# Last expert tile of a decoder block: sums moved between the halves of its gate and up products, the final scaling moved mostly to VectorE, and a drain on GpSimd's queue

## The chip, the cores and the metric

The kernel runs on one core of one Trainium2 chip. The metric is device time in microseconds: 1058.45 us is the median of three runs of the kernel before (1056.13 to 1059.59). In the text PE is TensorE, DVE is VectorE, ACT is ScalarE, POOL is GpSimd and SP is SyncE, which issues most of the DMAs. A name with a q behind it (POOLq, SPq) is the engine's queue, where instructions stand that set registers, wait, drain or issue DMAs.

## The reference

One decoder block for 512 tokens of 1024 channels: two attention branches side by side, then 64 routed experts and a shared one, then a root-mean-square norm. What the change touches is the end of the routed experts and the norm:

```python
def expert_block(xs):
    tok, g, e = xs
    xb = x_pad[tok]
    hb = jax.nn.silu(xb @ w_exp_gate[e]) * (xb @ w_exp_up[e])
    return (hb @ w_exp_down[e]) * g[:, None]
...
routed = jax.ops.segment_sum(yb.reshape(n_rows, D), row_tok, num_segments=T + 1)[:T]
...
x = x + gate_f * moe_ffn(...)
return rms_norm(x, g_final)
```

## The kernel before

The rows of all experts are packed into 33 tiles of 128 rows (a tile holds 32 to 128 rows of an expert). For each tile POOL gathers the 128 token rows with an indirect DMA (`fetch`, L1218) and copies their token numbers (`tokf`, L1222). PE turns the gathered rows over (`turn`), and `first` (L1242) multiplies them with the gate and up weights of the tile's experts, eight channel blocks k, all into one PSUM buffer `gu`. `hide` makes the hidden values from it (ACT's Silu, L1250, and a product on DVE, L1251), `turn_hidden` turns them over on PE (L1257) and copies them out of PSUM on ACT (L1258). `expert_out` is called for the two halves of the 1024 channels: PE's products with the down weights into a PSUM buffer `y` (L1274), DVE's scaling by gate value (`ys`, L1278), then the split of the result into a high part on ACT (`yH`, L155) and a low part on DVE (`yL`, L158).

The segment sum is a matrix product too: `spread` makes a one-hot matrix `oht` of tokens by rows, and `combine` (L1298 and L1299, 128x512 each) multiplies it with `yH` and `yL` for each block i of 128 tokens and each half of the channels; DVE adds the result to the running sum `acc` in SBUF (L1300). Tiles are combined in pairs; in front of the last tile one tile stands uncombined (`full`).

Last tile, before (L1393 to L1460). `first` runs through, the tile in front is combined for the first half of the channels, and the hidden values are turned. For the second half of the channels nothing goes through `acc` in SBUF: `seed(i)` puts `acc` into a PSUM buffer `fo` by a product with the identity (L1418) and adds the tile in front to it (L1412, L1413); the four seeds stand around the two halves of the last tile's down products. Then, for each block i of 128 tokens, `add_last(i)` combines the last tile into `acc` for the first half, squares and sums it on ACT (L1433), adds the last tile to `fo` for the second half, squares and sums that on ACT too, multiplies the first half with the final gain on DVE (L1440), adds up the two sums of squares (`fs`, L1442), and raises them to the power -1/2 on POOL (L1443). `store_last(i)` scales the second half from PSUM on DVE (L1446), the first half on ACT (L1448), and SP stores both to HBM (L1450). `store_last(i - 1)` is called behind `add_last(i)`.

The order of the instructions on PE and SP is the order of the code. That on DVE, ACT and POOL is chosen by a scheduler, which goes by its own estimate of when inputs are ready; once chosen it is fixed, and each engine works through its own queue in that order. Behind the last store stands a loop for experts that overflowed their rows (L1485); its count is read from the data, and here it is not entered. Then come the waits for all DMAs and the drains and barriers in which a program ends (recorded under L1517).

Of the kernel before, what the change touches and what calls it, by code (L numbers as in the profile page):

```python
# [10 lines left out]
F32 = mybir.dt.float32  # L11
# [75 lines left out]
def build(ctx, tc, a, out, dbg=None):  # L87
# [1128 lines left out]

    def fetch(T, x):
# [4 lines left out]
        follow(G.tensor_copy(tokf, tb[:, T, 0:1]), last[0])  # L1222
# [169 lines left out]

    T = TILES - 1  # L1393
# [10 lines left out]
    hid = hide(*first([ents], xT))  # L1404
    combine(full, cols=halves[:1])
    hT = turn_hidden(hid)
    sums = []

    def part(i, states, c, start, stop):
        t = slice(i * 128, (i + 1) * 128)  # L1410
        for q, (oht, yH, yL) in enumerate(states):
            PE.matmul(sums[i], oht[:, t], yH[:, c], start=start and q == 0, stop=False)  # L1412
            PE.matmul(sums[i], oht[:, t], yL[:, c], start=False, stop=stop and q == len(states) - 1)  # L1413

    def seed(i):
        tag, bufs = (("tr", 2), ("tr", 2), ("cb", 1), ("gu", GUB))[i]
        sums.append(mo_p.tile([128, S], F32, name="fo", tag=tag, bufs=bufs))
        PE.matmul(sums[i], ident, acc[:, i, halves[1]], start=True, stop=False)  # L1418
        part(i, full, halves[1], False, False)

    seed(0)
    state = spread(toks.pop(T))
    expert_out(0, T, ents, hT, state, WIDE)
    seed(1)
    expert_out(1, T, ents, hT, state, WIDE)
    seed(2)
    seed(3)
    outs = [xg[T % 3], xg[(T - 1) % 3]]
    outs += [work.tile([128, D], F32, name="yo", tag=tag, bufs=n) for tag, n in (("xT", 1), ("yH", 2))]

    def square(i, n, src):

        return A.activation(outs[i][:, halves[1]], src, AF.Square, scale=1.0 / 32.0, accum_out=fs[:, n, i:i + 1])  # L1433

    def add_last(i):
        combine([state], [i], ((("ht", 1), ("gu", GUB), ("ht", 1), ("y", 2))[i],), halves[:1])
        square(i, 0, acc[:, i, halves[0]])
        part(i, [state], halves[1], False, True)
        square(i, 1, sums[i])
        V.tensor_tensor(outs[i][:, halves[0]], acc[:, i, halves[0]], gfin[:, halves[0]], ALU.mult)  # L1440
        p = slice(i, i + 1)
# [3 lines left out]
    def store_last(i):  # L1445
        V.scalar_tensor_tensor(outs[i][:, halves[1]], sums[i], fs[:, 1, i:i + 1], gfin[:, halves[1]], op0=ALU.mult,  # L1446
                               op1=ALU.mult)
        scaled = A.mul(outs[i][:, halves[0]], outs[i][:, halves[0]], fs[:, 1, i:i + 1])  # L1448
        for c in halves[::-1]:
            SP.dma_start(outr[:, i, c], outs[i][:, c])  # L1450
        return scaled

    for i in range(NT):
        add_last(i)
        if i:
            store_last(i - 1)
# [73 lines left out]
```

## Time and profile before

| what | value |
| --- | --- |
| median of the runs, us | 1058.45 |
| lowest and highest run, us | 1056.13, 1059.59 |
| profiled execution, us | 1053.89 |
| its span, first to last instruction, us | 1052.2 |
| busy share PE, DVE, ACT, POOL | 95%, 55%, 30%, 15% |
| mean granted clock of PE, share of full speed | 0.981 |

The profiled execution is faster than each of the three runs; it has 1.7 us outside its span. A busy time is the sum over an engine's instructions. The chain of waits follows the work that ended last back to what released it. The 40 slices of the page show PE at 0.9 or more through nearly the whole span; the last slice, which holds the stores and the end of the program, has PE at 0.3.

### The profile page before, as it was taken

How to read it: one execution, taken by the hardware profiler on the slowest of the kernel's cores; microseconds unless marked ns; L12 is line 12 of the kernel's file. 1: busy time of each engine (PE TensorE's matmuls, PEld its weight loads, DVE VectorE, ACT ScalarE, POOL GpSimd, SP SyncE). 2: the span in 40 equal slices, each digit the busy share in tenths (PEclk: the TensorE clock that was granted, in tenths of full speed). 3: DMA queues.
4: the chain of work that ended last, by engine and by line, in shares of the span. 5: the costliest groups of instructions: out<-in, count | busy, mean ns of one | idle time of the engine just before them, and what ended most of it. 6: DMA issues, size and time to landing. Idle time of an engine off the chain costs nothing.

```text
span 1052.2 us, 16301 instructions
## 1 busy us (share of the span) xinstructions
PE 1001.2 (95%) x5904; PEld 602.8 (57%) x5904; DVE 575.1 (55%) x1151; ACT 320.5 (30%) x701; POOL 156.1 (15%) x209
## 2 busy tenths in 40 slices
PE   8999999998989988998899999999999999999993
PEld 7678667776756668975434444454344444434442
DVE  3568676477748653676344455454445455445454
ACT  3445553232225532430222222122212212222214
POOL 1513001000031265145200000000000000000000
PEclk8999999998999999999999999999999999999997
DMA  8942104599660276715699999999999999999782
GB/s 236 309 148 57 57 1 133 195 287 272 183 211 21 81 252 243 249 62 187 229 416 414 417 417 369 382 417 413 389 381 369 381 417 410 377 376 415 310 313 81
DMA packets 104467, 286.11 MB, mean 272 GB/s; under 512 B 18241, under 2 KB 65049, under 8 KB 80322
## 3 DMA queue, kind: packets, MB, share of 16 engines
q1 hardware_dynamic: 97458, 270.33, 69.0%
q0 software_dynamic: 5648, 12.63, 3.2%
q10 hardware_dynamic: 1280, 2.10, 0.7%
q8 instruction: 47, 0.77, 0.3%
q14 instruction: 34, 0.28, 0.1%
HBM read 282.46 MB, written 4.66 MB: 273 GB/s over the span
## 4 chain that ended last, share of the span: by engine, by line
PE 80%; DVE 6%; DMA 5%; SPq 3%; issue 2%; POOL 2%; ACT 1%; POOLq 0%; ACTq 0%; DVEq 0%
PE gu L1242 22%; PE y L1274 11%; PE o L150 6%; PE o L149 6%; PE o L151 6%; PE o L1298 6%; PE o L1299 5%; PE tp L1229 3%; PE sp L570 3%; PE oc L594 2%; PE tp L582 2%; DMA wm<-in_w_mod_dram 1%; PE og L1027 1%; PE tp L1257 1%; DMA w<-in_w_mod_dram 1%
## 5 line engine op out<-in xcount | busy, mean ns | idle before, releaser
L1242 PE MATMUL gu<-gu,xT 128*32 128x512 f32 (+1 forms) x1664 | 233.4, 594 | 0.0
L1242 PEld LDWEIGHTS gu<-gu,xT 128*32 128x32 f32 (+1 forms) x1664 | 69.1, 117 | 150.7 <-issue 137.0
L1274 PE MATMUL y<-dn,hid 128*32 128x512 f32 (+1 forms) x832 | 120.5, 596 | 0.0
L1251 DVE TENSOR_TENSOR hid<-hid,gu 128x256 f32<-128x256 f32 x33 | 13.9, 421 | 164.9 <-ACT hid L1250 164.9
L1298 PE MATMUL o<-yH,oht 128*128 128x512 f32 x256 | 101.9, 398 | 0.7 <-DVE acc L1300 0.7
L1300 DVE TENSOR_TENSOR acc<-acc,o 128x512 f32<-128x512 f32 x136 | 91.0, 686 | 17.4 <-PE o L1299 17.4
L1299 PE MATMUL o<-yL,oht 128*128 128x512 f32 x256 | 100.1, 391 | 0.0
L150 PE MATMUL o<-hH,wL 128*128 128x512 f32 x208 | 83.4, 401 | 1.2 <-DVE wL L158 1.2
L149 PE MATMUL o<-hH,wH 128*128 128x512 f32 x208 | 83.2, 400 | 0.0
L151 PE MATMUL o<-hL,wH 128*128 128x512 f32 x208 | 82.4, 396 | 0.0
L155 ACT CAST yH<-ys 128x512 fp32r<-128x512 f32 (+1 forms) x68 | 41.2, 607 | 109.3 <-DVE ys L1278 109.3
L158 DVE TENSOR_TENSOR yL<-ys,yH 128x512 fp32r<-128x512 f32 (+1 forms) x68 | 45.9, 677 | 43.5 <-ACT yH L155 43.3
L1274 PEld LDWEIGHTS y<-dn,hid 128*32 128x32 f32 (+1 forms) x832 | 32.5, 117 | 63.8 <-issue 54.6
L1250 ACT ACTIVATE hid<-gu 128x256 f32<-128x256 f32 x33 | 12.7, 386 | 180.4 <-PE gu L1242 180.4
L1278 DVE SCALAR_TENSOR_TENSOR ys<-y,tb,gmb 128x512 f32<-128x512 f32 (+1 forms) x68 | 49.8, 735 | 30.8 <-PE y L1274 26.8
L1218 POOL DMA_INDIRECT xg<-h2d,tb x22 | 22.2, 1011 | 274.5 <-PE tp L1229 191.5
L1298 PEld LDWEIGHTS o<-yH,oht 128*128 128x128 f32 x256 | 48.1, 188 | 12.9 <-DVE acc L1300 2.3
L898 ACT ACTIVATE xT<-tp,ab 128x128 f32<-128x128 f32 x132 | 49.8, 457 | 14.0 <-PE tp L1229 12.4
L1299 PEld LDWEIGHTS o<-yL,oht 128*128 128x128 f32 x256 | 48.1, 188 | 9.4
L900 DVE TENSOR_SCALAR xT<-tp,ab 128x128 f32<-128x128 f32 x132 | 45.2, 405 | 10.2 <-ACT xT L898 7.4
L149 PEld LDWEIGHTS o<-hH,wH 128*128 128x128 f32 x208 | 39.5, 190 | 12.0 <-issue 1.9
L150 PEld LDWEIGHTS o<-hH,wL 128*128 128x128 f32 x208 | 39.6, 191 | 11.4 <-DVE wL L158 1.8
(384 smaller groups left out, 1673.5 us busy)
## 6 DMA issues: line engine op xcount, KB each, us to landing
gu<-in_w_exp_gate_dram SPq DMA_DIRECT2D x63, 1024.0 KB
gu<-in_w_exp_up_dram SPq DMA_DIRECT2D x63, 1024.0 KB
dn<-in_w_exp_down_dram SPq DMA_DIRECT2D x60, 1024.0 KB
w<-in_w_mod_dram SPq DMA_DIRECT2D x32, 512.0 KB
w<-in_w_in_dram SPq DMA_DIRECT2D x13, 1024.0 KB
wm<-in_w_mod_dram SPq DMA_DIRECT2D x16, 512.0 KB
wraw<-in_w_out_dram SPq DMA_DIRECT2D x12, 512.0 KB
dn<-in_w_exp_down_dram SPq DMA_DIRECT2D x8, 512.0 KB
```

Source lines behind the costliest of these rows:

```text
L149: PE.matmul(o, l[0], r[0], start=start, stop=False)
L150: PE.matmul(o, l[1], r[0], start=False, stop=False)
L151: return PE.matmul(o, l[0], r[1], start=False, stop=stop)
L158: return le.tensor_tensor(L, src, f(H), ALU.subtract)
L898: A.activation(out, src, AF.Identity, bias=ab2[:, 1, k:k + 1], scale=ab2[:, 0, k:k + 1])
L900: V.tensor_scalar(out, src, ab2[:, 0, k:k + 1], ab2[:, 1, k:k + 1], op0=ALU.mult, op1=ALU.add)
L1242: last[0] = PE.matmul(gu[lo:lo + n], xT[:, k, lo:lo + n], w[:, :, k], start=(k == 0), stop=(k == KD - 1))
L1274: last[0] = PE.matmul(y[lo:lo + m], hT[:, j, lo:lo + m], w[:, j, c], start=(j == 0), stop=(j == 1))
L1278: V.scalar_tensor_tensor(ys[:, b], y[:, b], f(tb[:, T, 1:2]), gfb[:, c][:, b], op0=ALU.mult, op1=ALU.mult)
L1298: m = PE.matmul(o, oht[:, i * 128:(i + 1) * 128], yH[:, c], start=(q == 0), stop=False)
L1299: PE.matmul(o, oht[:, i * 128:(i + 1) * 128], yL[:, c], start=False, stop=(q == len(state) - 1))
L1300: d = V.tensor_tensor(acc[:, i, c], acc[:, i, c], o, ALU.add)
```

## The change

Four things are changed, all in the last tile.

- `first` is called twice for the last tile, for k 0 to 3 and for k 4 to 7, into the same PSUM buffer. Between the calls the tile in front is combined for the first half of the channels; behind the second call it is combined for the second half too, now also through `acc` in SBUF (`combine`, with DVE's additions).
- The seeds with their two products each are gone from between the down products. Each block's `fo` now gets `acc` by the identity and then the last tile's two products, all behind the down products of both halves; the four combinations of the first half stand in front of all of these.
- In `store_last` the first half of blocks 0 to 2 is scaled on DVE in one instruction with the final gain, in place of a product on DVE and a scaling on ACT; block 3 keeps the old form. Stores of blocks 0 to 2 go out first half first. The scheduler is switched off for DVE, ACT and POOL behind the down products, so the order there is that of the code.
- A drain is put on POOL's queue behind the last gather's copy of token numbers.

```diff
@@ -1214,12 +1214,15 @@
         q, e = late.pop(0)
         WT[q][1] = load_dn(where[q], e)
 
+    last_fetch = [None]
+
     def fetch(T, x):
         last[0] = G.indirect_dma_start(out=x, out_offset=None, in_=h2d,
                              in_offset=bass.IndirectOffsetOnAxis(ap=tb[:, T, 0:1], axis=0),
                              bounds_check=S - 1, oob_is_err=False)
         tokf = work.tile([128, 1], F32, name="tokf", bufs=6)
-        follow(G.tensor_copy(tokf, tb[:, T, 0:1]), last[0])
+        last_fetch[0] = G.tensor_copy(tokf, tb[:, T, 0:1])
+        follow(last_fetch[0], last[0])
         return tokf
 
     def turn(x, xT, parts=range(2)):
@@ -1390,6 +1393,7 @@
 
 
 
+
     T = TILES - 1
     ents, xT = todo.pop(T)
     late_dn = []
@@ -1401,60 +1405,63 @@
             SP.dma_start(to[:, :, c], src[:, :, c])
     fs = work.tile([128, 2, NT], F32, name="fs")
     outr = out[0].rearrange("(i p) d -> p i d", p=128)
-    hid = hide(*first([ents], xT))
+    dr = G.drain()
+    follow(dr, last_fetch[0])
+    gu, = first([ents], xT, range(0, 4))
     combine(full, cols=halves[:1])
+    hid = hide(*first([ents], xT, range(4, KD), gu))
+    combine(full, cols=halves[1:])
     hT = turn_hidden(hid)
-    sums = []
-
-    def part(i, states, c, start, stop):
-        t = slice(i * 128, (i + 1) * 128)
-        for q, (oht, yH, yL) in enumerate(states):
-            PE.matmul(sums[i], oht[:, t], yH[:, c], start=start and q == 0, stop=False)
-            PE.matmul(sums[i], oht[:, t], yL[:, c], start=False, stop=stop and q == len(states) - 1)
-
-    def seed(i):
-        tag, bufs = (("tr", 2), ("tr", 2), ("cb", 1), ("gu", GUB))[i]
-        sums.append(mo_p.tile([128, S], F32, name="fo", tag=tag, bufs=bufs))
-        PE.matmul(sums[i], ident, acc[:, i, halves[1]], start=True, stop=False)
-        part(i, full, halves[1], False, False)
-
-    seed(0)
     state = spread(toks.pop(T))
-    expert_out(0, T, ents, hT, state, WIDE)
-    seed(1)
-    expert_out(1, T, ents, hT, state, WIDE)
-    seed(2)
-    seed(3)
+    for n in range(2):
+        expert_out(n, T, ents, hT, state, WIDE)
+    oht, yH, yL = state
     outs = [xg[T % 3], xg[(T - 1) % 3]]
     outs += [work.tile([128, D], F32, name="yo", tag=tag, bufs=n) for tag, n in (("xT", 1), ("yH", 2))]
+    sums = []
 
     def square(i, n, src):
 
-        return A.activation(outs[i][:, halves[1]], src, AF.Square, scale=1.0 / 32.0, accum_out=fs[:, n, i:i + 1])
+        A.activation(outs[i][:, halves[1]], src, AF.Square, scale=1.0 / 32.0, accum_out=fs[:, n, i:i + 1])
 
     def add_last(i):
-        combine([state], [i], ((("ht", 1), ("gu", GUB), ("ht", 1), ("y", 2))[i],), halves[:1])
+        combine([state], [i], ((("cb", 1), ("gu", GUB), ("ht", 1), ("gu", GUB))[i],), halves[:1])
         square(i, 0, acc[:, i, halves[0]])
-        part(i, [state], halves[1], False, True)
+
+    def sum_last(i):
+        c, t, p = halves[1], slice(i * 128, (i + 1) * 128), slice(i, i + 1)
+        sums.append(mo_p.tile([128, S], F32, name="fo", tag=("tr", "tr", "y", "y")[i]))
+        PE.matmul(sums[i], ident, acc[:, i, c], start=True, stop=False)
+        PE.matmul(sums[i], oht[:, t], yH[:, c], start=False, stop=False)
+        PE.matmul(sums[i], oht[:, t], yL[:, c], start=False, stop=True)
         square(i, 1, sums[i])
-        V.tensor_tensor(outs[i][:, halves[0]], acc[:, i, halves[0]], gfin[:, halves[0]], ALU.mult)
-        p = slice(i, i + 1)
+        if i == NT - 1:
+            V.tensor_tensor(outs[i][:, halves[0]], acc[:, i, halves[0]], gfin[:, halves[0]], ALU.mult)
         V.scalar_tensor_tensor(fs[:, 0, p], fs[:, 0, p], EPS, fs[:, 1, p], op0=ALU.add, op1=ALU.add)
         G.tensor_tensor(fs[:, 1, p], fs[:, 0, p], mh[:, 0:1], ALU.pow)
 
     def store_last(i):
-        V.scalar_tensor_tensor(outs[i][:, halves[1]], sums[i], fs[:, 1, i:i + 1], gfin[:, halves[1]], op0=ALU.mult,
-                               op1=ALU.mult)
-        scaled = A.mul(outs[i][:, halves[0]], outs[i][:, halves[0]], fs[:, 1, i:i + 1])
-        for c in halves[::-1]:
+        r, c = fs[:, 1, i:i + 1], halves[0]
+        if i == NT - 1:
+            A.mul(outs[i][:, c], outs[i][:, c], r)
+        else:
+            V.scalar_tensor_tensor(outs[i][:, c], acc[:, i, c], r, gfin[:, c], op0=ALU.mult, op1=ALU.mult)
+        c = halves[1]
+        scaled = V.scalar_tensor_tensor(outs[i][:, c], sums[i], r, gfin[:, c], op0=ALU.mult, op1=ALU.mult)
+        for c in halves if i < NT - 1 else halves[::-1]:
             SP.dma_start(outr[:, i, c], outs[i][:, c])
         return scaled
 
+    tail_order = tc.manual_schedule(engines={getattr(mybir.EngineType, e) for e in MAN})
+    tail_order.__enter__()
     for i in range(NT):
         add_last(i)
+    for i in range(NT):
+        sum_last(i)
         if i:
             store_last(i - 1)
     scaled = store_last(NT - 1)
+    tail_order.__exit__(None, None, None)
     order.__exit__(None, None, None)
     for i in range(NT):
         follow(A.copy(acc[:, i, halves[1]], sums[i]), scaled)
```

The first place is on PE, around the turn of the hidden values (tp) and the down products (y) of the last tile; o is `combine`, fo the sums of the second half. Before:

```order
L1299 MATMUL o<-yL,oht 128x512
L1257 MATMUL tp<-ident,hid 128x128 x2
L1418 MATMUL fo<-acc,ident 128x512
L1412 MATMUL fo<-yH,oht 128x512
L1413 MATMUL fo<-yL,oht 128x512
L1274 MATMUL y<-dn,hid 32x512 x8
L1418 MATMUL fo<-acc,ident 128x512
```

In the changed kernel, at the same place on PE, with the last product of `combine` in front of it and the first two of the next behind it:

```order
L1302 MATMUL o<-yL,oht 128x512
L1260 MATMUL tp<-ident,hid 128x128 x2
L1277 MATMUL y<-dn,hid 32x512 x16
L1301 MATMUL o<-yH,oht 128x512
L1302 MATMUL o<-yL,oht 128x512
```

The three products that stood between the turn and the down products are gone, and the down products of both halves now follow each other.

The second place is on DVE, from the last addition to `acc` on: fs is the sums of squares, hs, xg1 and the two yo are the output rows of blocks 0 to 3 (yo_9624 and yo_9625 before, yo_9625 and yo_9626 in the changed kernel), xg0 holds the final gain. Before, where the scheduler chose:

```order
L1442 SCALAR_TENSOR_TENSOR fs_9515<-fs_9515 128x1
L1440 TENSOR_TENSOR xg1_3453<-acc_3448,xg0_3452 128x512
L1446 SCALAR_TENSOR_TENSOR hs_3451<-fo_9572,fs_9515,xg0_3452 128x512
L1440 TENSOR_TENSOR yo_9624<-acc_3448,xg0_3452 128x512
L1442 SCALAR_TENSOR_TENSOR fs_9515<-fs_9515 128x1
L1300 TENSOR_TENSOR acc_3448<-acc_3448,o_9667 128x512
L1442 SCALAR_TENSOR_TENSOR fs_9515<-fs_9515 128x1
L1446 SCALAR_TENSOR_TENSOR xg1_3453<-fo_9596,fs_9515,xg0_3452 128x512
L1440 TENSOR_TENSOR yo_9625<-acc_3448,xg0_3452 128x512
L1446 SCALAR_TENSOR_TENSOR yo_9624<-fo_9616,fs_9515,xg0_3452 128x512
```

In the changed kernel, on DVE from its last addition to `acc` to its last scaling:

```order
L1303 TENSOR_TENSOR acc_3448<-acc_3448,o_9644 128x512
L1440 SCALAR_TENSOR_TENSOR fs_9515<-fs_9515 128x1 x2
L1448 SCALAR_TENSOR_TENSOR hs_3451<-acc_3448,fs_9515,xg0_3452 128x512
L1450 SCALAR_TENSOR_TENSOR hs_3451<-fo_9649,fs_9515,xg0_3452 128x512
L1440 SCALAR_TENSOR_TENSOR fs_9515<-fs_9515 128x1
L1448 SCALAR_TENSOR_TENSOR xg1_3453<-acc_3448,fs_9515,xg0_3452 128x512
L1450 SCALAR_TENSOR_TENSOR xg1_3453<-fo_9656,fs_9515,xg0_3452 128x512
L1439 TENSOR_TENSOR yo_9626<-acc_3448,xg0_3452 128x512
L1440 SCALAR_TENSOR_TENSOR fs_9515<-fs_9515 128x1
L1448 SCALAR_TENSOR_TENSOR yo_9625<-acc_3448,fs_9515,xg0_3452 128x512
L1450 SCALAR_TENSOR_TENSOR yo_9625<-fo_9667,fs_9515,xg0_3452 128x512
L1450 SCALAR_TENSOR_TENSOR yo_9626<-fo_9678,fs_9515,xg0_3452 128x512
```

The last addition to `acc` (o_9667 before, o_9644 now) has moved in front of all scalings, and two scalings of each of blocks 0 to 2 stand together, behind the sum of squares of the next block.

## Rows read from the trace of the kernel before

**Rows 1.** Busy time by stretch: PE, PEld, DVE, ACT, POOL, clock, DMA share, GB/s.
```profile
1035.00:1040.00 5.00, 0.82 (x4) 0.36 (x2) 4.53 (x11) 4.33 (x13) 2.04 (x3) 1.00 0.29 108
1040.00:1041.00 1.00, 0.00 (x0) 0.00 (x0) 0.53 (x1) 1.00 (x3) 0.00 (x0) 0.74 0.88 334
```

**Rows 2.** Timeline of the last block: start us, us, engine, line, operation, what came before.
```profile
1040.37 0.58 ACT L1433 ACTIVATE yo<-fo 128x512 f32<-128x512 f32 x1
1040.85 0.19 ACT L1433 ACTIVATION_READ_ACCUMULATOR yo<-fo 128x1 f32 x1
1041.07 0.16 DVE L1442 SCALAR_TENSOR_TENSOR fs<-fs 128x1 f32<-128x1 f32 x1 [0.55 <-ACT yo L1433]
1041.32 0.55 POOL L1443 TENSOR_TENSOR fs<-fs,mh 128x1 f32<-128x1 f32 x1 [2.17 <-DVE fs L1442]
1041.90 0.75 DVE L1446 SCALAR_TENSOR_TENSOR yo<-fo,fs,xg 128x512 f32<-128x512 f32 x1 [0.66 <-POOL fs L1443]
```

**Rows 3.** Line 1517, end of the program: times in ns min/median/max, first and last start.
```profile
L1517 POOLq DRAIN  x3: 40/103/5063, 1046.2 to 1051.8; - x3
L1517 SPq DRAIN  x3: 7/7/113, 1046.9 to 1051.8; - x3
```

**Rows 4.** Line 1511, start of the program.
```profile
L1511 POOLq INC_SWDGE_SEM  x1: 27/27/27, 0.2 to 0.2; - x1
L1511 POOLq DRAIN  x1: 169/169/169, 0.4 to 0.4; - x1
```

**Rows 5.** Page, part 3: packets, MB and share of the queue that POOL issues to.
```profile
q0 software_dynamic: 5648, 12.63, 3.2%
```

**Rows 6.** Line 1485, the loop that isn't entered.
```profile
L1485 POOLq INC_SWDGE_SEM  x1: 1404/1404/1404, 1042.4 to 1042.4; - x1
```

**Rows 7.** Timeline of POOL, last gather and first power.
```profile
946.28 1.01 POOL L1218 DMA_INDIRECT hs<-h2d,tb  x1 [10.77 <-PE tp L1229]
...
1035.45 0.95 POOL L1443 TENSOR_TENSOR fs<-fs,mh 128x1 f32<-128x1 f32 x1 [87.97 <-DVE fs L1442]
```

**Rows 8.** Chain of waits, last tile: start us, us, engine, tile, line.
```profile
1013.42 6.87 PE gu L1242 x64
1020.28 0.43 PE o L1298
1020.71 0.23 PE o L1299
...
1022.57 0.22 PE tp L1257 x2
1022.79 0.86 PE fo L1418 x2
...
1024.11 1.85 PE y L1274 x16
1025.97 1.06 PE fo L1418 x2
```

**Rows 9.** Timeline, DVE and ACT beside these products.
```profile
1021.11 2.47 DVE L1300 TENSOR_TENSOR acc<-acc,o 128x512 f32<-128x512 f32 x4
1022.83 0.37 ACT L1258 COPY hid<-tp 128x256 f32<-128x256 f32 x1 [2.09 <-PE tp L1257]
1026.04 0.88 DVE L1278 SCALAR_TENSOR_TENSOR ys<-y,tb,gmb 128x256 f32<-128x256 f32 x2 [2.46 <-PE y L1274]
1027.05 0.76 DVE L158 TENSOR_TENSOR yL<-ys,yH 128x256 fp32r<-128x256 f32 x2
```

**Rows 10.** Timeline, pace of ACT's squares and of DVE's scalings and products.
```profile
1035.37 0.62 ACT L1433 ACTIVATE yo<-acc 128x512 f32<-128x512 f32 x1
...
1035.98 0.58 ACT L1433 ACTIVATE xg<-fo 128x512 f32<-128x512 f32 x1
...
1038.52 0.75 DVE L1446 SCALAR_TENSOR_TENSOR xg<-fo,fs,xg 128x512 f32<-128x512 f32 x1
...
1039.18 0.68 DVE L1440 TENSOR_TENSOR yo<-acc,xg 128x512 f32<-128x512 f32 x1
```

## The prediction

> **What bounds the kernel now.** I read the busy time by stretch first. Up to the last tile PE has work in every microsecond, and the change leaves the amount of that work as it is, so what can be won lies behind PE's last product. The reader is to see in [rows 1] that PE has 0.82 us of work left at 1035, that DVE (4.53 of 5 us) and ACT (4.33 of 5 us) are then nearly full, and that from 1040 on little runs at all. The timeline of the last block [rows 2] shows how the results end: square, its accumulator, sum on DVE, power on POOL, last scaling, done at 1041.90 + 0.75 = 1042.65. But the span ends at 1052.2, 9.5 us later. So I looked at the line on which the program ends [rows 3]: POOL's queue holds a drain of 5.06 us. SP's drain, the other engine's end that can be read there, starts at 1046.9 and takes 0.11. POOL's first drain starts at 1046.2 and so ends at 1051.26, about 4.25 us behind SP. The barrier that follows waits for all engines, so the end of the program waits for that drain, and the remaining 0.9 us of barriers come behind it.
>
> There are thus two terms: the tail from PE's products to the last store, and POOL's drain.
>
> **The change part by part.**
>
> *PE.* The number of products is the same: 64 rows of gate and up, 16 of the tile in front, 16 + 16 down, 16 of the last tile, 4 identities. What moves is where PE changes between narrow products (32 wide) and wide ones. In [rows 8] the first wide product behind narrow ones costs 0.43 for 0.23, so 0.20; the same shows in 1.06 for an identity behind y against 0.86 elsewhere. Narrow ones behind wide ones: 16 rows of y take 1.85, while 16 at the pace of gate and up (6.87 / 64 = 0.107) take 1.72, so 0.13. Before there are three changes to wide and two back; afterwards three and two. Nothing is won or lost there.
>
> The times then go: gate and up, first half, from 1013.42, 3.43, to 1016.85. Eight sums, 0.20 + 8 x 0.23 = 2.04, to 1018.9. Second half 0.13 + 3.43, to 1022.45. The next eight sums stand where before eight stood, right behind gate and up and beside the same Silu and product; there they took from 1020.28 to 1022.57, 2.29 with their small stall, so they end at 1024.75. The turn of the hidden values, 0.22, ends at 1024.97. Now comes the one new wait on PE: the copy on ACT that took 0.37 and started 0.04 behind the turn [rows 9] was covered by a seed (0.86 and two products); this cover is gone, so the down products start at about 1025.4, 0.4 later than they could. Queued behind them are all sums of the last tile. They run 0.13 + 2 x 1.72 = 3.57, to 1028.97. The first half's high and low parts were ready 1.84 behind its product (1025.97 to 1027.81 in [rows 8, 9]), so at 1025.4 + 1.85 + 1.84 = 1029.1, and the four combinations (0.20 + 8 x 0.23) run to 1031.0. Each block's `fo` then costs 0.86 + 2 x 0.23 = 1.32: they end at 1032.3, 1033.65, 1034.95 and 1036.3. PE is done at 1035.8 before [rows 1], so PE ends 0.5 later.
>
> *DVE, in front of the tail.* Four additions are new. Four of them take 2.47 [rows 9] and run beside the sums and the down products: they start 0.83 behind the end of gate and up as before (1020.28 to 1021.11), so at 1023.3, and end at 1025.8, 1.4 before the first down product is done. They cost nothing; without that cover they would cost 2.5. The last four end later: DVE's two scalings of the second half run from 1029.0 to 1029.9, the first addition to 1030.6 (0.62 each), the low parts to 1031.35 (0.76), three additions to 1033.25.
>
> *ACT.* It loses three scalings. Its queue now holds the four squares of the first half, then the four of `fo`. The fourth starts at 1033.3, when the last addition is done. Squares follow each other at 0.61 (1035.37 to 1035.98, [rows 10]), so block 0's second square starts at 1033.9, block 1's at 1034.5. A square starts 0.70 before its sum on DVE (1040.37 to 1041.07, [rows 2]): sums at 1034.6 and 1035.2. Block 0's power starts at 1034.85 and takes 0.95, as the first one does [rows 7], and the first scaling starts at 1035.8.
>
> *DVE, the tail.* From there it is DVE's queue that ends last. Scalings follow each other at 0.66 (1038.52 to 1039.18, [rows 10]). Two scalings 1.32, a sum 0.16, two scalings 1.32, block 3's product 0.66, a sum 0.16, two scalings 1.32, the last scaling 0.75: 5.69, so 1041.5. The power of block 3 (0.55) and ACT's scaling beside it are done before. Against 1042.65 that is **1.16 us earlier**. The stores go out a block at a time as before, and ACT's four last copies end before the last store has landed. If the first power takes 0.55 and the squares keep up, it is 0.4 better. If the down products start 1 us later than I have it, 1 us is lost. The two ends that I keep for this term: 0.5 us lost, 2.4 won.
>
> *The drain.* What it costs where it is put: it stands behind the last gather, which ended at 947.3, and POOL then has nothing to do for 87.97 us [rows 7]. Even a drain of 5.06 us is hidden there, and nothing is queued behind it but the four powers. What it takes away is not shown by the trace of before: the final drain in a program whose POOL has been drained in between. The bounds are 5.06 (nothing changes) and about 0.1 (the drains that follow it at once take 0.04 and 0.10). The nearest row is the drain at the program's start [rows 4]: 0.17 us, with POOL's fills still running, but with no DMA issued by POOL yet. Between the two POOL has issued DMAs of 5648 packets [rows 5]. The last gather was issued 100 us before 1046.2, and the code waits for all DMAs in front of its final drains, so the 5.06 us are no wait for a transfer; I take them for work that the DMAs issued by POOL have left behind, and that an earlier drain does in the idle stretch. Behind the last gather POOL issues no DMA. So I take 0.17. What is late next is SP: 1046.9 - 1.16 + 0.11 = 1045.85, against POOL's 1051.26.
>
> The Trainium skill ("VectorE: DVE Perf Modes", section on the drain that can't be avoided) speaks against this term: it says that the drains of a program's start and end are boilerplate of about 12 ns on all five engines, the same for every kernel. By it a drain put earlier takes nothing away, and only the 1.16 us are left. The trace doesn't agree for POOL: 169 ns and 5063 ns [rows 3, 4]. SP's is 113 ns at the longest.
>
> **The sum.** 1051.26 - 1045.85 = 5.4 us, of which 1.16 from the tail and 4.25 from the drain. The profiled execution would go from 1053.89 to 1048.5. It lies 4.6 below the median of the runs; the terms don't depend on what makes an execution faster, so against the median the forecast is 1058.45 - 5.4 = **1053.0**.
>
> **The rivals.**
>
> *The final drain keeps its length.* Then the tail's 1.16 is all: 1057.3. For it speaks that an operation on POOL's DMA semaphores takes 1.40 us just before the end, at 1042.4 [rows 6], behind the new drain; if that leaves the work behind, an early drain can't do it. Against it: the same operation at the start took 0.03 and the drain behind it 0.17 [rows 4].
>
> *DVE's new additions are not covered.* If the first scaling of the last tile waits behind them for their whole 2.5, the tail is 1.3 slower than before, and with the drain's 4.25 the time is 1055.5. It decides whether the fourth addition ends after the first down product (1027.25); I have 1.4 us between.
>
> *The clock.* PE now stands still before the down products. If its granted clock fell there from 2.4 to 1.2 GHz, the products behind it (3.57 + 2.04 + 5.28 = 10.9 us) would take twice as long: 10.9 lost, 5.4 won, 1063.9, slower than before even with the drain gone. The point is how long PE stands still: 0.4 us by my count. Against it: PE's last product ends at 1035.8, the clock is still 1.00 up to 1040 and falls only behind it (0.74, [rows 1]).
>
> **How the numbers follow.** Forecast 0.65, drain keeps its length 0.25, additions not covered 0.06, clock 0.04. The three runs of before lie within 3.5 us, so medians of three can differ by 1 or 2 us with no change; a difference of 0.3%, 3.2 us, is about what can be told. The forecast's own range is 1051.0 to 1055.0 (the tail's ends, and the runs). The drain's rival stands at 1057.3 give or take 1; the range takes it in for the most part: 1050.8 to 1058.0. Faster by over 0.3% means under 1055.3: nearly all of the forecast (0.63), half of the third case (0.03), a little of the drain's rival (0.02), together 0.68. Slower by over 0.3%: the clock, and a tail that comes out worse in the drain's rival, 0.06. Within 0.3%: 0.26.
>
> **What would show it.** In the changed kernel's profile: a drain on POOL's queue near 947, of some us, and a first drain at the end under 0.3 us; the span ending about 6 us behind the last scaling, not 9.5. A final drain of 5 us makes the forecast wrong whatever the tail does. For the tail: down products starting near 1025.4, PE's last product near 1036.3, the last scaling on DVE at 1041.5 with DVE hardly idle from 1035.8 on. If DVE waits there for ACT's squares or for POOL's powers, the tail's size is wrong.

## The result

The changed kernel takes 1050.15 us (median of six runs, 1047.62 to 1053.97); the kernel before, in the runs beside it, takes 1057.48 (six runs, 1053.87 to 1059.59). The ratio is 0.9941, with a 95% interval of 0.992 to 0.9961: 4 to 8.5 us faster. The predicted saving, 5.4 us, lies inside; the predicted 1053.0 us lies above the median, one microsecond of it because the kernel before itself came out at 1057.48 and not at 1058.45. The medians are 7.3 us apart. The profiles below account for 5.3 us of that, and in a second timing of the same kernel (experiment 10) the medians are 5.1 us apart, so the rest lies within the spread of the runs.

The profiled execution of the changed kernel is the slowest of its six runs (1053.97 us). Its span is 1052.2 us, the same as before: executions differ by more than the effect, so spans can't be compared. One event stands in all profiles ahead of all that the change touches on PE, DVE and ACT (only the drain, on POOL, lies before it): the start of the last tile's first gate and up product, at 1013.42 before [rows 8] and at 1018.83 now. Everything below is counted from it, and called "from the last tile's start". From there to the end of the span it was 38.74 us before; it is 33.41 now, 5.3 less.

The end of the program comes first. These are the rows of the early drain, of the loop that isn't entered and of the program's end, in the kernel after: times in ns (min/median/max), first and last start.

```profile
L1408 POOLq DRAIN  x1: 11636/11636/11636, 949.8 to 949.8; - x1
...
L1492 POOLq INC_SWDGE_SEM  x1: 173/173/173, 1045.7 to 1045.7; - x1
...
L1524 POOLq DRAIN  x3: 34/43/103, 1050.6 to 1051.9; - x3
L1524 SPq DRAIN  x3: 7/7/113, 1051.3 to 1051.9; - x3
```

Against [rows 3] the 5063 ns are gone from the end, and against [rows 6] the operation on the semaphores fell from 1404 to 173 ns. POOL's first drain starts at 1050.6 and none takes more than 0.103 us, so at 1051.3, when SP's first one starts, it is done: SP now ends last. The early drain is longer than the one it replaces, 11.6 us, but it ends at 961.4, and POOL's next operation starts at 1040.44, 79 us later. From the last scaling to the end of the span it was 9.51 us; it is 5.74.

Then the tail. The chain that ended last, in the kernel after (start us, us, what):

```profile
1024.44 3.57 PE gu L1245 x32
1028.01 0.43 PE o L1301
...
1030.29 0.23 PE tp L1260 x2
1030.52 0.02 issue
1030.55 0.38 ACT hid L1261
1030.93 0.04 issue
1030.97 3.64 PE y L1277 x32
```

To be seen: the second half of gate and up, the sums of the tile in front behind it, the turn, and then PE waiting for ACT's copy of the hidden values, which a seed had covered before [rows 8, 9]. Counted from the last tile's start, the down products start at 12.14; the prediction had 12.0.

The timeline of POOL, ACT and DVE in the kernel after (start us, us, engine, line, operation, idle before and who ended it):

```profile
1040.44 1.12 POOL L1441 TENSOR_TENSOR fs<-fs,mh 128x1 f32<-128x1 f32 x2 [89.25 <-DVE fs L1440]
1042.60 0.99 POOL L1441 TENSOR_TENSOR fs<-fs,mh 128x1 f32<-128x1 f32 x1 [1.04 <-DVE fs L1440]
...
1045.62 0.72 ACT L1446 ACTIVATE yo<-yo,fs 128x512 f32<-128x512 f32 x1 [2.87 <-POOL fs L1441]
...
1032.96 0.88 DVE L1281 SCALAR_TENSOR_TENSOR ys<-y,tb,gmb 128x256 f32<-128x256 f32 x2 [1.66 <-PE y L1277]
...
1036.90 1.87 DVE L1303 TENSOR_TENSOR acc<-acc,o 128x512 f32<-128x512 f32 x3
1040.19 0.16 DVE L1440 SCALAR_TENSOR_TENSOR fs<-fs 128x1 f32<-128x1 f32 x1 [1.42 <-ACT hs L1425]
1040.77 0.16 DVE L1440 SCALAR_TENSOR_TENSOR fs<-fs 128x1 f32<-128x1 f32 x1 [0.42 <-ACT xg L1425]
1041.04 0.75 DVE L1448 SCALAR_TENSOR_TENSOR hs<-acc,fs,xg 128x512 f32<-128x512 f32 x1
1041.71 0.74 DVE L1450 SCALAR_TENSOR_TENSOR hs<-fo,fs,xg 128x512 f32<-128x512 f32 x1
1042.38 0.15 DVE L1440 SCALAR_TENSOR_TENSOR fs<-fs 128x1 f32<-128x1 f32 x1
1042.44 0.74 DVE L1448 SCALAR_TENSOR_TENSOR xg<-acc,fs,xg 128x512 f32<-128x512 f32 x1
...
1043.77 0.68 DVE L1439 TENSOR_TENSOR yo<-acc,xg 128x512 f32<-128x512 f32 x1
...
1044.43 0.74 DVE L1448 SCALAR_TENSOR_TENSOR yo<-acc,fs,xg 128x512 f32<-128x512 f32 x1
1045.10 1.40 DVE L1450 SCALAR_TENSOR_TENSOR yo<-fo,fs,xg 128x512 f32<-128x512 f32 x2
```

DVE works without a gap from the first scaling at 1041.04 to the end of the last at 1046.50; ACT idles 2.87 us. The last scaling ends 27.67 us from the last tile's start, against 29.23 before [rows 2, 8], so 1.56 earlier. Not all of that reaches the end. By stretch (columns as in [rows 1]), the kernel after:

```profile
994.00:998.00 4.00, 4.00 (x21) 1.03 (x24) 0.49 (x1) 0.84 (x2) 0.00 (x0) 0.57 0.76 303
...
1035.00:1040.00 5.00, 5.00 (x19) 3.10 (x17) 3.77 (x8) 3.91 (x12) 0.00 (x0) 1.00 0.00 0
...
1046.00:1047.00 1.00, 0.00 (x0) 0.00 (x0) 0.49 (x1) 1.00 (x3) 0.00 (x0) 0.50 1.01 383
1047.00:1048.00 1.00, 0.00 (x0) 0.00 (x0) 0.00 (x0) 1.00 (x3) 0.00 (x0) 0.50 1.03 383
1048.00:1049.00 1.00, 0.00 (x0) 0.00 (x0) 0.00 (x0) 0.27 (x1) 0.00 (x0) 0.50 0.86 326
```

From 1046 to 1048 all 16 DMA engines are busy with stores (share 1.01 and 1.03, 383 GB/s). The four halves of the last two blocks are scaled from 1044.43 to 1046.50; their four stores carry 4 x 128 x 512 x 4 bytes = 1.05 MB, and at 383 GB/s that is 2.7 us. The last packet ends 2.91 us behind the last scaling, against 2.36 before, when block 2's second half was ready 2.1 us ahead of block 3's. So 0.55 of the 1.56 is given back. Full engines are not all of it. The packets in the trace (2 KB each, 0.08 us of an engine's time) show that here one engine ends 0.44 us behind all others, with the last packets to itself; before, the last two engines end within 0.02 us of each other.

The first of these rows shows one thing more: in this execution the clock was at 0.57 on average from 994 to 998 (for 3.4 of these 4 us at 0.5, the level of 1.2 GHz), during the gate and up products of the tile in front. PE had worked 3.69 of the 4 us before. They took 8.8 us, not 7.1: 1.7 of the 5.4 us by which this profile's last tile starts late. The other 3.7 us lie ahead of the last gather. Experiment 10 asks whether they belong to the change.

### The profile page after: what moved, and what is told of

Same layout as the page of the kernel before. It is cut to its first block, busy times and chain, and to the rows that moved or that the text cites. A ratio compares the mean times of both kernels' runs of the same rounds, so it can differ in the third digit from the quotient of the medians.

```text
span 1052.2 us, 16304 instructions
## 1 busy us (share of the span) xinstructions
PE 1002.3 (95%) x5904; PEld 601.2 (57%) x5904; DVE 577.6 (55%) x1155; ACT 317.8 (30%) x698; POOL 154.8 (15%) x209
## 4 chain that ended last, share of the span: by engine, by line
PE 79%; DVE 6%; DMA 6%; SPq 3%; POOL 2%; issue 2%; ACT 2%; ACTq 0%; POOLq 0%; DVEq 0%
PE gu L1245 22%; PE y L1277 11%; PE o L1301 6%; PE o L1302 6%; PE o L150 6%; PE o L149 5%; PE o L151 5%; PE tp L1232 3%; PE sp L570 3%; PE oc L594 2%; PE tp L582 2%; DMA w<-in_w_mod_dram 2%; DMA wraw<-in_w_out_dram 1%; SPq L237 1%; PE tp L1260 1%
## 5 line engine op out<-in xcount | busy, mean ns | idle before, releaser
L1303 DVE TENSOR_TENSOR acc<-acc,o 128x512 f32<-128x512 f32 x140 | 93.2, 683 | 17.4 <-PE o L1302 17.4
```

What stands on the lines that cost most here:

```text
L1303: d = V.tensor_tensor(acc[:, i, c], acc[:, i, c], o, ALU.add)
```

## The experiments

All profiles in one table, in us. The last tile's start is counted from the span's start; the next three columns are counted from the last tile's start. "Landed" is the end of the last packet of the stores. The upper five rows are the kernel before and its variants, the lower seven the changed kernel and its variants.

| kernel | last tile's start | to last scaling | to landed | to end of span | landed behind last scaling | first drain at the end, POOL |
| --- | --- | --- | --- | --- | --- | --- |
| before | 1013.42 | 29.23 | 31.59 | 38.74 | 2.36 | 5.06 |
| 1 drain alone | 1020.12 | 29.24 | 31.60 | 34.41 | 2.36 | 0.04 |
| 4 three drains | 1016.38 | 29.22 | 31.58 | 34.40 | 2.36 | 0.06 |
| 5 drain 40 us later | 1017.54 | 29.20 | 31.58 | 34.41 | 2.38 | 0.04 |
| 8 drain in the tail | 1014.57 | 32.87 | 35.24 | 38.08 | 2.38 | 0.04 |
| after | 1018.83 | 27.67 | 30.58 | 33.41 | 2.91 | 0.04 |
| 10 after, again | 1014.66 | 27.68 | 30.93 | 33.78 | 3.25 | 0.04 |
| 2 without drain | 1016.67 | 27.67 | 30.65 | 37.80 | 2.98 | 5.06 |
| 3 scalings shared | 1015.09 | 26.26 | 30.67 | 33.50 | 4.41 | 0.04 |
| 7 first halves on ACT | 1014.89 | 26.84 | 31.45 | 34.30 | 4.61 | 0.04 |
| 6 order by the scheduler | 1012.20 | 27.07 | 29.92 | 32.78 | 2.85 | 0.04 |
| 9 the same, timed | 1012.24 | 27.08 | 30.06 | 32.89 | 2.98 | 0.04 |

**1. The drain alone.** The kernel before with nothing but the drain.

```diff
+        last_fetch[0] = G.tensor_copy(tokf, tb[:, T, 0:1])
+        follow(last_fetch[0], last[0])
...
+    dr = G.drain()
+    follow(dr, last_fetch[0])
     hid = hide(*first([ents], xT))
```

> The kernel before with one edit: the drain on POOL's queue behind the last gather. Two stretches are read in its profile: the tail (first gate and up product of the last tile to the end of the last scaling: 29.2 us in the kernel before, 27.7 in the changed one) and the end (from there to the end of the span: 9.5 and 5.7). Theory A (the drain does early the work that POOL's DMAs have left behind): tail 29.2, end 5.7, about 3.8 us faster than the kernel before. Rival B (the end is shorter for another reason, such as the new order of the stores): tail 29.2, end 9.5, no faster.

1051.07 us against 1056.49 for the kernel before, ratio 0.9948 (0.9931 to 0.9965). The tail is that of before to 0.01 us; the span ends 4.33 us earlier from the last tile's start. The drains of this kernel (columns as above):

```profile
L1407 POOLq DRAIN  x1: 11156/11156/11156, 951.1 to 951.1; - x1
...
L1522 POOLq DRAIN  x3: 34/43/103, 1052.9 to 1054.2; - x3
```

The drain does its work by itself: the predicted 4.25.

**2. Everything but the drain.** The changed kernel without `dr = G.drain()`.

```diff
-    dr = G.drain()
-    follow(dr, last_fetch[0])
```

> The changed kernel without the drain: sums and scalings as changed. Theory A: tail 27.7, end 9.5 with a last drain of about 5 us, so about 1.5 us faster than the kernel before, which can hardly be told in time from no change. Rival B: end 5.7, some 5 us faster. On the powers on POOL: if the drain has to do with their lengths, the first takes 0.95 again; if a DVE operation with two inputs in SBUF beside them makes them long, the pattern of the changed kernel (0.56, 0.56, 0.99, 0.99) stays.

1054.52 us, ratio 0.9978 (0.9962 to 0.9994). The end as it was:

```profile
L1522 POOLq DRAIN  x3: 40/103/5063, 1048.5 to 1054.1; - x3
L1522 SPq DRAIN  x3: 7/7/113, 1049.2 to 1054.1; - x3
```

The long drain is back to the nanosecond. The tail alone is worth 0.94 us at the end of the span, and 0.94 + 4.33 = 5.27 is the 5.33 of the whole change: the parts add up. The powers take 0.57, 0.54, 0.99 and 0.99 us as in the changed kernel, so the drain has nothing to do with their lengths.

**3. Scalings shared between DVE and ACT.** Block 2's and 3's gain products go into DVE's idle 1.42 and 0.42 us, their scalings to ACT's idle 2.87 us, and ACT's squares of blocks 2 and 3 between those of `fo`.

```diff
+    gain(3)
+    sum_last(0)
+    power(0)
+    gain(2)
...
+        if n == 0 and i >= 2:
+            return A.mul(outs[i][:, c], outs[i][:, c], r)
```

> The changed kernel with the tail's order changed again: DVE multiplies blocks 2 and 3 with the final gain in the 1.8 us in which it waited for ACT's squares, ACT scales both blocks, and ACT's squares of blocks 0 and 1 of the second half stand in front of those of blocks 2 and 3 of the first half. If DVE's queue behind the first sum of squares sets the tail, as the prediction had it, the first scaling starts 1 us earlier and DVE has two scalings fewer behind it: last scaling 2.0 us earlier, tail 25.7, end 5.7, about 7.4 us faster than the kernel before. Rival: the last block's own chain (its sums on PE, square, sum, power, scaling) sets the end; then at most 1.5 us are won, tail 26.2 or more.

1051.0 us, ratio 0.9953 (0.9938 to 0.9968): no better than the changed kernel, and the 7.4 us expected are not there. The last scaling does come 1.41 us earlier (at 26.26, where 25.7 was expected), but the span ends 0.09 later. The rival's 26.2 fits by its number and not by its reason: DVE has no gap between its scalings from 1036.90 on, so its queue still sets the last one. Of the missing 0.56 us, 0.38 is POOL's first power, 0.94 us and not 0.57, because DVE's gain product of block 2 runs beside it. By stretch:

```profile
1042.00:1043.00 1.00, 0.00 (x0) 0.00 (x0) 0.00 (x0) 1.00 (x3) 0.00 (x0) 0.53 1.01 379
1043.00:1044.00 1.00, 0.00 (x0) 0.00 (x0) 0.00 (x0) 0.26 (x1) 0.00 (x0) 0.50 1.04 387
1044.00:1045.00 1.00, 0.00 (x0) 0.00 (x0) 0.00 (x0) 0.00 (x0) 0.00 (x0) 0.50 0.57 209
1045.00:1046.00 1.00, 0.00 (x0) 0.00 (x0) 0.00 (x0) 0.00 (x0) 0.00 (x0) 0.50 0.05 18
```

DVE has no work left in these rows. The DMA engines are full until past 1044: the stores of blocks 2 and 3 are issued within 1.7 us of each other, and landing takes 4.41 us instead of 2.91. So behind a certain point the tail is bound by the stores, not by what makes their data.

The last row shows something else: a share of 0.05, about one engine in 16. By the packets 14 engines are done at 1044.63, one at 1045.12, and the last one works alone until 1045.76. In all seven kernels with the changed tail one 16 KB packet of a queue of the kind `instruction` (part 3 of the profile's page) takes 0.9 to 1.6 us of an engine's time among the stores; in the five with the tail of before it ends about when the first store's packets begin. It may be what puts one engine back, but the packets don't name their engine, and in experiment 9 no engine is late (0.02 us) though the packet is there. The cause of the late engine stays open.

**4. Is the long drain a backlog of all the DMAs?** The kernel before with a drain behind gathers 11, 22 and 33.

```diff
+        if T in (10, 21, 32):
+            dr = G.drain()
+            follow(dr, tc_)
```

> The kernel before with three drains on POOL's queue, behind gathers 11, 22 and 33 (the last). In front of the first stand 24 scatters, 4 plain DMAs and 11 gathers, in front of the second and third 11 gathers each. In the changed kernel the only one takes 11.6 us. Theory A (work grows with the DMAs since the drain before): the first is the longest, the second and third are equal and under half of it, the last drain of the program under 0.2. Rival C (a drain waits for the gather in flight, and the work behind it is the same whatever the count): three equal drains. Rival D (a cost of the first drain alone): the first 5 us or more, the others 0.2 or the length of the gather in flight.

One run, 1052.55 us.

```profile
L1230 POOLq DRAIN  x3: 9595/10086/10330, 605.5 to 947.3; - x3
...
L1527 POOLq DRAIN  x3: 52/60/103, 1049.1 to 1050.4; - x3
```

Three drains of nearly one length, as in rival C, though the first has the 24 scatters of the routing table, 4 plain DMAs and 11 gathers behind it and the others 11 gathers each. But most of each length is the gather in flight. Taken apart at the gather's last packet:

| drains right behind a gather | POOL's DMAs since the drain before | from POOL's last operation to the gather's last packet, us | from that packet to the drain's end, us |
| --- | --- | --- | --- |
| 4, first | 39 | 6.75 | 2.15 |
| 4, second and third | 11, 11 | 7.70, 7.22 | 0.95, 0.94 |
| 1, 3, 6, 7, 9, 10 and after, the only one | 61 (all) | 6.70 to 7.23 | 2.99 to 3.04 |

The last column is the same to 0.05 us wherever the count is the same, and it grows with the count: about 0.04 us for each DMA. The second and third drain of experiment 4 have equal rests, under half of the first's, as theory A had it for the whole. So the work that is left when the gather has landed does grow with the number of DMAs since the last drain; the whole lengths hide it. The end is as short as with one drain.

**5. How much of it is waiting for the last gather?** In the changed kernel the last gather is issued at 949.99 and its packets move from 954.2 to 958.4; the drain ends at 961.4. Here the drain comes some 40 us later, when nothing is in flight from POOL.

```diff
         if T == TILES - 4:
+            probe = work.tile([128, 1], F32, name="probe", bufs=1)
+            dr = G.drain()
+            follow(dr, G.tensor_copy(probe, f(full[-1][1][:, 0:1])))
```

> The kernel before with the drain on POOL's queue about 40 us behind the last gather (behind a small copy on POOL that waits for a result of the fourth tile from the end). Three drains behind a gather took 9.6 to 10.3 us each whatever stood in front of them, one 99 us behind the last gather 5.06. Rival C, now the theory (a drain waits until a gather in flight has landed, and has about 5 us of work of its own that does not depend on the count): about 5.1 us here, the last drain of the program 0.1, end 5.1 to 5.7 us. Rival E (the drain is slow in the stretch of the tiles because DVE and the DMAs are busy beside it): 9 us or more here too.

One run, 1053.73 us.

```profile
L1384 POOLq DRAIN  x1: 5812/5812/5812, 992.0 to 992.0; - x1
...
L1520 POOLq DRAIN  x3: 34/43/103, 1050.3 to 1051.6; - x3
```

The record of a drain starts while POOL is still at its operation in front. Here that is the small copy, which ends at 992.73; from there the drain takes 5.09 us, the 5.06 of the program's end (61 DMAs in front of both). Rival E falls. In the changed kernel the operation in front is the copy of the token numbers:

```profile
949.99 1.01 POOL L1220 DMA_INDIRECT hs<-h2d,tb  x1 [10.77 <-PE tp L1232]
950.99 0.20 POOL L1224 CAST tokf<-tb 128x1 f32<-128x1 int32 x1
```

It ends at 951.19, and the drain 10.2 us later: 5.1 more than with nothing in flight. Since only 3.0 of the 10.2 lie behind the last packet, some 2 of the 5.09 seem to be done while the gather is still in flight. The expectation's "does not depend on the count" isn't shown here: every drain with nothing in flight had all 61 DMAs in front of it.

**6. The order left to the scheduler.** The changed kernel without the order by hand in the tail.

```diff
-    tail_order = tc.manual_schedule(engines={getattr(mybir.EngineType, e) for e in MAN})
-    tail_order.__enter__()
...
-    tail_order.__exit__(None, None, None)
```

> The changed kernel with the scheduler left on for DVE, ACT and POOL in the tail. DVE's order then differs in one thing: the product of block 3 with the final gain stands behind the first sum of squares, in a stretch in which DVE waited, and one scaling has changed places with a sum. If DVE's queue behind the first power sets the tail: 0.6 earlier, tail 27.1 against 27.7. If the order written by hand is what made the tail shorter than before: tail 28.5 to 29.2.

One run, 1046.71 us. From the last tile's start the last scaling comes 0.60 us earlier than in the changed kernel, as expected if DVE's queue sets the tail, and the end 0.63. The rest of the low time is the early start of the last tile, 1012.20. DVE:

```profile
1035.72 0.75 DVE L1448 SCALAR_TENSOR_TENSOR xg<-acc,fs,xg 128x512 f32<-128x512 f32 x1 [0.66 <-POOL fs L1441]
1036.39 0.15 DVE L1440 SCALAR_TENSOR_TENSOR fs<-fs 128x1 f32<-128x1 f32 x1
...
1037.20 0.75 DVE L1448 SCALAR_TENSOR_TENSOR yo<-acc,fs,xg 128x512 f32<-128x512 f32 x1
1037.87 1.40 DVE L1450 SCALAR_TENSOR_TENSOR yo<-fo,fs,xg 128x512 f32<-128x512 f32 x2
```

Block 3's gain product is done ahead of all scalings here, while in the changed kernel it stands between them (1043.77, 0.68 us).

**7. First halves on ACT again.** The changed kernel with the scaling of all four first halves as before: product on DVE, scaling on ACT.

```diff
-        if i == NT - 1:
+        if True:
             V.tensor_tensor(outs[i][:, halves[0]], acc[:, i, halves[0]], gfin[:, halves[0]], ALU.mult)
...
-        if i == NT - 1:
+        if True:
             A.mul(outs[i][:, c], outs[i][:, c], r)
```

> The changed kernel with the first halves of all four blocks scaled on ACT again (a product with the final gain on DVE, then the scaling on ACT), in the written order. DVE has as many operations, but two of the products stand in front of the first power, where DVE waited; ACT gets three scalings more (0.72 each), behind its squares. If the move of the scalings to DVE is worth something: tail longer than 27.7, 28.5 or more. If not (the gain comes from the sums and from the order): about 1.2 us shorter, 26.5.

One run, 1050.92 us. DVE's last scaling comes 0.83 us earlier (at 26.84, near the 26.5 expected if the move is worth nothing there), but the end 0.89 later. ACT's last scaling is issued at 1040.98 and its four copies follow; the stores:

```profile
1041.00:1042.00 1.00, 0.00 (x0) 0.00 (x0) 0.73 (x1) 1.00 (x2) 0.00 (x0) 1.00 0.52 191
1042.00:1043.00 1.00, 0.00 (x0) 0.00 (x0) 0.00 (x0) 1.00 (x3) 0.00 (x0) 0.55 1.02 385
1043.00:1044.00 1.00, 0.00 (x0) 0.00 (x0) 0.00 (x0) 0.63 (x2) 0.00 (x0) 0.50 1.04 385
1044.00:1045.00 1.00, 0.00 (x0) 0.00 (x0) 0.00 (x0) 0.00 (x0) 0.00 (x0) 0.50 1.02 379
```

As in experiment 3: four stores come at once behind 1041 and keep the DMA engines full for three microseconds, and behind that two engines end late, by 0.4 and 1.0 us. So the scaling on DVE doesn't make the last scaling earlier. Whether it is worth the 0.89 us at the end by letting blocks finish one after the other, as may be, one execution doesn't show: 0.6 of it is the late engine.

**8. The drain where POOL has work.** The kernel before with the drain between the first and the second power.

```diff
-        G.tensor_tensor(fs[:, 1, p], fs[:, 0, p], mh[:, 0:1], ALU.pow)
+        pw = G.tensor_tensor(fs[:, 1, p], fs[:, 0, p], mh[:, 0:1], ALU.pow)
+        if i == 0:
+            dr[0] = G.drain()
+            follow(dr[0], pw)
+        elif i == 1:
+            follow(pw, dr[0])
```

> The kernel before with the drain between the first and the second power on POOL, where nothing covers it and nothing is in flight from POOL. Theory: the drain takes about 5.1 us; the second power starts 5.1 us behind the end of the first, not 1.5, and the scalings behind it are late by 3.5 or some less for the last block: tail 31.5 to 32.7 against 29.2; the last drain is 0.1 long and the end 5.1 to 5.7, so that only 1 to 2 us of the 4.3 are left. If the drain were 0.2 here, the tail would stay at 29.2 and the last drain at 5.06.

One run, 1054.41 us. POOL in the tail:

```profile
1036.61 0.95 POOL L1445 TENSOR_TENSOR fs<-fs,mh 128x1 f32<-128x1 f32 x1 [89.67 <-DVE fs L1444]
1042.74 1.06 POOL L1445 TENSOR_TENSOR fs<-fs,mh 128x1 f32<-128x1 f32 x2 [5.18 <-issue]
```

The drain's record is 6.08 us long and starts beside the first power; from that power's end at 1037.56 the drain takes 5.09. The second power waits for it, and the last scaling is 3.64 us late (32.87 against 29.23), a little over the range expected. The end of the program gains its 4.3 all the same, so the span ends only 0.66 us earlier. The same drain is free in the idle stretch and costs nearly all that it brings where work is queued behind it.

**9. and 10. The scheduler's order and the changed kernel, timed together.** The edit of experiment 6, and the changed kernel as it is.

> The changed kernel with its tail's hand-written order taken away (the kernel of e6), now timed in rounds. Theory: e6's one look, 1046.71 us, holds two things apart: its end is 0.63 us shorter than the changed kernel's from the last tile's first gate and up product to the end of the span (32.78 against 33.41), and the rest, some 3.5 us, is the start of that product, which differs from run to run and has nothing to do with the tail. So it comes out 0.4 to 0.9 us below the changed kernel in the same rounds, at a ratio of 0.993 to 0.9945 to the kernel before. Rival: the order changes the work ahead of the tail as well, and the kernel keeps most of e6's lead: 3 us or more below the changed kernel.

> The changed kernel itself, timed again beside e9 and in the same rounds. Theory: the 5 us before the last tile that its profiled execution had lost (1018.83 against 1013.42 for the first gate and up product of the last tile) belong to that execution: this profile has that product between 1012 and 1016, a span of 1045.5 to 1049.5 us, and from that product to the end of the span 33.4 us again, within 0.4; the ratio to the kernel before is 0.993 to 0.996. Rival: the drain behind the last gather, or the new order, costs time ahead of the last tile: the product starts at 1018 or later again.

Experiment 9: 1050.25 us (1044.09 to 1055.11, twelve runs), ratio 0.9953 (0.9929 to 0.9977). Experiment 10: 1050.45 us (1047.2 to 1055.8, twelve runs), ratio 0.9958 (0.994 to 0.9977). The tail is 0.9 us shorter by the profiles and the median 0.2 lower, where 0.4 to 0.9 was expected: runs that spread over 8 to 11 us can't tell these two apart, and the rival's 3 us are not there. So a better version than the changed kernel is seen in the profile but not shown in the time.

Experiment 10's last tile (chain):

```profile
1012.94 1.72 PE y L1277 x16
1014.66 3.43 PE gu L1245 x32
```

It starts at 1014.66, not at 1018.83. In the table kernels with and without the drain start it anywhere from 1012.20 to 1020.12; the changed kernel has had both 1014.66 and 1018.83. Nothing here ties the late start to the change: it goes by the execution. What makes it vary ahead of the last gather was not looked into and stays open.

## Why the prediction was right, and where not

The mechanism and both signs hold. By its own steps, times counted from the last tile's start:

- *PE.* Down products forecast at 12.0, measured 12.14; PE's end forecast 22.9, measured 23.1 (1041.96). The wait for ACT's copy is 0.45 where 0.4 was forecast, and the clock stays at 1.00 from 1035 to 1040 behind it. The clock's rival falls. (The 0.57 of the result section is in another tile and not in experiment 10.)
- *DVE's new additions.* Behind the last of them DVE idles 1.66 us until the first down product is done (1.4 forecast). That rival falls too.
- *DVE's tail.* 5.69 forecast from first to last scaling, measured 5.46: a sum of squares has 0.15 as its duration, but the scaling behind it starts 0.06 later. The first scaling is 0.2 earlier than forecast. The last scaling is thus 1.56 earlier than before, against 1.16. Of the three parts of the tail's change this points to the moved sums: with the scalings on ACT again or the order left to the scheduler the last scaling comes earlier still (experiments 7 and 6). But no run has the moved sums alone.
- *The first power.* The step "takes 0.95, as the first one does" was wrong: in the changed kernel the powers of blocks 0 and 1 take 0.57 and 0.54, those of blocks 2 and 3 0.99. In all twelve profiles a power takes 0.94 to 1.02 where DVE is already in an operation with both inputs in SBUF (the 0.95 at 1036.61 in experiment 8, the 0.99 at 1042.60 beside the scaling of 1042.44), and 0.54 to 0.57 otherwise. The Trainium skill ("SBUF — State Buffer", section "Who interferes with whom") states such a rule: a DVE instruction with two SBUF inputs contends with a GpSimd instruction that reads SBUF. The change moved such operations of DVE onto the powers of blocks 2 and 3; it costs nothing yet, because the last power ends 0.2 us before the scaling that needs it.
- *The stores.* "The stores go out a block at a time as before" is the step that failed: it puts at nothing what landing costs more. Behind the last scaling the stores land 0.55 us later (0.6 and 0.9 in experiments 2 and 10), so the tail is worth 1.01 (after), 0.94 and 0.66 us, not 1.56 or the forecast 1.16. What lies behind it are full DMA engines, and one engine that ends 0.44 or 0.45 us behind the others in each of these three profiles; why it is late stays open (experiment 3).
- *The drain.* 4.25 forecast, 4.33 measured alone. The rival in which the final drain keeps its length is what experiment 2 shows without the early drain; with it, it falls. For the drain that is left 0.17 was taken; it is 0.04, and none of the three at the end is over 0.10.
- *Its cause.* "Work that the DMAs issued by POOL have left behind" holds as far as the runs go. An early drain takes it over; it is no wait for transfers (5.09 us with nothing in flight, experiments 5 and 8); and what is left of a drain behind a gather's last packet grows with the DMAs since the drain before (experiment 4). What POOL does in it no run shows. Not foreseen was that a drain right behind a gather also ends only behind its last packet, 10 us in all; the 88 idle us cover both.
- *The 12 ns.* What the prediction cites of the Trainium skill ("VectorE: DVE Perf Modes", section "The DRAIN you can't avoid") doesn't hold for POOL here: 5063 ns for the first drain of the end without an early drain, and 43 ns with one.

The sum came out at 5.3 (33.41 against 38.74) and 5.0 in experiment 10, for 5.4 forecast: 0.4 too little in the scalings, 0.6 to 0.9 too much in the landing. That it came so close is in part luck: two errors of opposite sign.

## What to carry to other kernels

Look behind the last store: if POOL has issued DMAs and the profile shows a drain of microseconds on its queue at the program's end, put a drain behind POOL's last DMA where POOL has over 10 us with nothing to do. Where the last blocks are scaled and stored, count the stores: past the point where the DMA engines are full, a faster scaling is given back while landing; and look at the last microsecond, where a share near 1/16 is one engine that ends late. And compare two profiles from a common event near the change, not from the span, when the executions spread by more than the effect.

## What the runs showed of the hardware

- POOL's drain takes 0.17 us at the start, when POOL has issued no DMA. Counted from the end of POOL's operation in front of it, where one is still at work, it takes 5.06 to 5.09 us behind 61 DMAs that have landed, and 8.2 to 10.2 us right behind a gather, of which 0.94 to 3.04 us lie behind the gather's last packet, more with more DMAs since the drain before. At the end it takes 0.03 to 0.10 us when an earlier drain has run. The operation on POOL's DMA semaphores falls with it from 1404 to 173 ns.
- SP's drain at the end starts about 1.9 us behind the last packet of the last store (1045.01 to 1046.9 before, 1049.41 to 1051.3 after, 1045.76 to 1047.6 in experiment 3).
- Four stores of 262 KB at once run at 379 to 387 GB/s with all 16 DMA engines busy (after, experiments 3 and 7).
- A power of 128x1 on POOL takes 0.94 to 1.02 us where DVE is already in an operation with both inputs in SBUF, 0.54 to 0.57 otherwise (48 powers in twelve profiles).
